# Attention items in ten steps, one step an iteration, with negated keys

## The chip, the cores and the metric

The kernel runs on one core of a Trainium2 chip. The metric is device time in microseconds (us) of one execution, the median of several; lower is better. In what follows PE is the matmul engine (TensorE), DVE is VectorE, ACT is ScalarE, POOL is GpSimd and SP issues the transfers (DMAs).

## What is computed

One block of an encoder over 1024 tokens of width 1024. Three branches mix the tokens, a merge and an output projection follow, and then sixteen experts. The change touches the two attention branches and what runs beside them:

```
# neighbourhood attention: 16 rows x 64 columns of tokens, 6 heads of 64
scores = einsum(q_r * dh**-0.5, k_win) + bias         # window 8 x 16 around each token
probs  = softmax(scores)
out    = einsum(probs, v_win)
# memory attention: 1024 tokens against 256 memory rows, 4 heads of 64
probs  = softmax(einsum(qh * dh**-0.5, kh));  out = einsum(probs, vh)
# the recurrent branch ends with a group norm over each head
y = ((y_sum - mean) * rsqrt(var + eps)) * ln_g + ln_b + bonus_sum;  y = y * g
merged = sum over the branches of sigmoid(gate) * (y_branch @ w_branch)
```

## The kernel before, in words

The program is a row of stages. A recurrent scan with projections beside it comes first; then the attention stage; then the merge of the three branches (helper `mm3`, L235 to L237), the output projection with the router, and the experts, whose weights take more than half of the time. Each stage uses its own buffers, partly at the addresses of the stage before, so the first loads of the merge (its weights, L1077, and its gates, L1110) wait until the buffers they land on are free.

The attention stage is written under a manual schedule: the order in which the Python loop calls the operations is the order on every engine. There are 40 items: 24 of neighbourhood attention (3 pairs of heads, 8 groups of 128 tokens) and then 16 of memory attention (2 pairs of heads, 8 groups). One item is two heads times 128 queries, and goes through these steps:

- score: six matmuls into `s` (PSUM, two banks an item, two buffers). For a neighbourhood item DVE then adds the bias and takes the row maximum in one custom instruction a head (L954, 288 or 384 keys), for a memory item it reduces 2x256 scores to two maxima (L1019). A small DVE instruction (L956, L1020) changes the maxima's sign.
- exp: ACT computes exp(score - maximum) with its row sum, one instruction a head (L908).
- recip: DVE inverts the two sums (L911).
- trans: PE transposes the probabilities into `tr` (L963, L1029), and ACT and DVE copy them out to `pt` (L967, L965, L1030).
- mix: PE multiplies by the values into `av` (L972, L1035; one PSUM bank, one buffer) and spreads the reciprocal sums over 64 rows by a small matmul (L920); ACT copies these to `rb` (L922).
- out: DVE forms y = av * rb (L926), ACT writes its rounded part `yh` (L928), POOL the remainder `yl` (L929).

The table `PIPE` says which step of which item an iteration calls, and in which order. Before, an iteration n does the out of item n-4, the exp of n-1, the recip and trans of n-2, the mix of n-3 and the score of n. So trans and mix of different items, and out and mix, meet in one iteration.

Two more things are threaded into the loop. Side generators prepare the next heads (`na_load`, `mem_load`: loads, a split of keys and queries into two parts on ACT and POOL, transposes of the values). The generator `group_norm` runs the recurrent branch's norm in six pieces, and is advanced twice an iteration from iteration 2 on. Its matmuls are the centring one (L816), the sums of squares (L822), the transposes of the inverse norm (L832) and the gate (L838); POOL adds the two directions (L808, L809), the bonus (L836), and writes the remainder of the result (L844).

Of the kernel before, what the change touches and what calls it, by code (L numbers as in the profile page):

```python
# [56 lines left out]
PIPE = (("out", 4), ("exp", 1), ("recip", 2), ("trans", 2), ("mix", 3), ("score", 0))  # L57
# [103 lines left out]
def block_kernel(ctx: ExitStack, tc: tile.TileContext, T, out, dbg=None, upto=99):  # L161
# [514 lines left out]
    def fill_gen():  # L676
        jobs = []
        for j0, j1, fn, sc_, dst in ((11, 14, AF.Copy, 0.125, pna[0:3]), (14, 17, AF.Copy, 1.0, pna[3:6]), (17, 20, AF.Copy, 1.0, pvc),
                                     (20, 22, AF.Copy, 0.125, pmq), (22, 46, AF.Tanh, 0.5, pgt)):
            jobs += [(j, fn, sc_, dst[j - j0]) for j in range(j0, j1)]  # L680
# [14 lines left out]
        def evac():  # L695
            while pend:
                p, n, s0 = pend.pop()
                _, fn, sc_, dst = jobs[n]
                if n == 3:
                    split_to(*(t[:, s0:s0 + 512] for t in kt0), p)  # L700
                    continue
# [84 lines left out]
    def group_norm():  # L786
# [17 lines left out]
        yield  # L804
        for n, (t0, j) in enumerate(its):
# [10 lines left out]
            PE.matmul(pcb, C("cent"), y0, start=True, stop=True)  # L816
            A.activation(y1, pcb, AF.Copy)
# [3 lines left out]
            for i in range(4):  # L821
                PE.matmul(pn[:, 2 * i:2 * i + 2], b1[:, i * 128:(i + 1) * 128], C("hsel"), start=True, stop=True)  # L822
            rn = gq.tile([128, 8], F32, name="grn", bufs=2)
# [7 lines left out]
            for i in range(4):  # L831
                PE.transpose(pb[:, i * 128:(i + 1) * 128], rb[:, 2 * i:2 * i + 2].rearrange("p h t -> p (h t)"), ident)  # L832
            V.tensor_mul(y1, y1, pb)
# [4 lines left out]
            PE.matmul(pg, g2[:, j * 128:(j + 1) * 128], lg[:, t0:t0 + 512], start=True, stop=True)  # L838
            yield
# [9 lines left out]
    def bias_load(m):  # L849
        if m < 6:  # L850
            bias[m] = ap.tile([128, 2, BOFF[3]], F32, name="bias", bufs=3)
            SP.dma_start(bias[m], T["rpb"][m // 2, m % 2])

    def na_load(j):
# [32 lines left out]
        for cg in range(4):  # L887
            p = abank("tr")
            w = NCOL[CTYPE[cg]]
            for i in range(4):  # L890
                PE.transpose(p[:4 * w, i * 128:(i + 1) * 128], VW[cg][:, 4 * i * w:4 * (i + 1) * w], ident)
            src, dst = p[:4 * w].rearrange("p (i c) -> p i c", i=4), VT[:4 * w, cg]
            if cg % 2:
                V.tensor_copy(dst, src)
                yield
            else:
                A.activation(dst, src, AF.Copy)

    def attention(score_of, trans_of, mix_of, tokens):
        o = {}  # L900

        def score():
            o["st"] = ap.tile([128, 8], F32, name="st", bufs=4)
            score_of(o)

        def exp():
            for h in range(2):
                A.activation(o["sb"][h], o["e"][h], AF.Exp, bias=o["st"][:, 2 + h:3 + h], scale=1.0, accum_out=o["st"][:, 4 + h:5 + h])  # L908

        def recip():  # L910
            V.reciprocal(o["st"][:, 6:8], o["st"][:, 4:6])  # L911

        def trans():
            trans_of(o)

        def mix():
            o["av"] = av = abank("av")
            mix_of(o, av)
            for h, q in enumerate((LO, UP)):
                PE.matmul(av[q, 128:256], o["st"][:, 6 + h:7 + h].to_broadcast([128, 64]), ident, start=True, stop=True)  # L920
            o["rb"] = rb = ap.tile([128, 128], F32, name="rb", bufs=2)
            A.activation(rb, av[:, 128:256], AF.Copy)  # L922

        def out():
            y = ap.tile([128, 128], F32, name="y", bufs=3)
            V.tensor_mul(y, o["av"][:, 0:128], o["rb"])  # L926
            y = tokens(y)
            A.activation(tokens(yh), y, AF.Copy)  # L928
            G.tensor_tensor(tokens(yl), y, tokens(yh).bitcast(F32), op=OP.subtract)  # L929
# [3 lines left out]
    def na_item(j, g):  # L933
# [11 lines left out]
        def score(o):  # L945
            KT, qb = na[j][:2]
            s, st = abank("s"), o["st"]
            for i, (a, b) in enumerate(((0, 0), (1, 0), (0, 1))):
                for h, q in enumerate((LO, UP)):
                    PE.matmul(s[:, h, :n], qb[a][q, rh, cg], grid(KT[b][q])[:, r0:r0 + NROW, c0:c0 + w], start=(i == 0), stop=(i == 2))  # L950
            sb = ap.tile([128, 2, 384], F32, name="sb", bufs=4)
            o["e"] = o["sb"] = [sb[:, h, :n] for h in range(2)]
            for h in range(2):
                V.tensor_tensor_reduce(out=sb[:, h, :n], in0=s[:, h, :n], in1=bias[2 * j + rh][:, h, b0:b0 + n],  # L954
                                       scale=1.0, scalar=-3.0e38, op0=OP.add, op1=OP.max, accum_out=st[:, h:h + 1])
            V.tensor_scalar(st[:, 2:4], st[:, 0:2], -1.0, None, op0=OP.mult)  # L956

        def trans(o):
            o["pt"] = pt = ap.tile([128, 2, 384], F32, name="pt", bufs=3)
            for h in range(2):  # L960
                p = abank("tr")
                for k in range(3):
                    PE.transpose(p[:m, k * 128:(k + 1) * 128], o["sb"][h][:, k * m:(k + 1) * m], ident)  # L963
                if h:
                    V.tensor_copy(pt[:m, h], p[:m, :384])  # L965
                else:
                    A.activation(pt[:m, h], p[:m, :384], AF.Copy)  # L967
# [7 lines left out]
        return attention(score, trans, mix, tokens)  # L975

    kb = [ap.tile([128, 2, NM], F32R, name=f"kb{v}") for v in "hl"]
    qm, vms = [], []

    def mem_load():  # L980
# [7 lines left out]
        A.activation(kb[0], kv[:, 0:2], AF.Copy)  # L988
        G.tensor_tensor(kb[1], kv[:, 0:2], kb[0].bitcast(F32), op=OP.subtract)
# [3 lines left out]
        for j in range(2):  # L993
# [5 lines left out]
            if j == 0:  # L999
                for m in range(2):  # L1000
                    p = abank("tr")
# [520 lines left out]
```

## Time and profile before

| | us |
|---|---|
| median of 3 runs | 2385.06 (2382.33 to 2385.69) |
| the profiled execution | 2382.75 |
| its span in the profile | 2380.9 |
| attention stage, first score to first matmul of the merge | 842.80 to 1018.60 |
| PE busy, share of the span | 94% |
| DVE, ACT, POOL busy | 70%, 55%, 26% |

The span runs from the first instruction to the last; 1.85 us of the execution lie outside it. A busy share is an average over stages, and the attention stage is where PE's share is lowest. In the rows below a bracket at the end of a line gives how long the engine sat idle before it, and what ended that.

### The profile page before, as it was taken

To read this page: it belongs to the slowest core of one execution; us is meant where nothing else is said; L and a number is where in the kernel's file an instruction comes from. 1 tells how busy PE (TensorE), PEld (TensorE's weight loads), DVE (VectorE), ACT (ScalarE), POOL (GpSimd) and SP (SyncE) were. 2 spreads that over 40 slices of the span, in tenths; PEclk is the share of its full clock that TensorE was granted. 3 is DMA by queue.
4 is the path that set the end of the run, shared out by engine and by line. 5 is a ranking of instruction groups with operands and counts; after the bars stand their busy time and mean duration, and the time that the engine had idled before them with its cause. 6 is when DMAs were issued, how large, how long until landed. Compare 5 with 4: busy or idle time off the path is not lost.

```text
span 2380.9 us, 33660 instructions
## 1 busy us (share of the span) xinstructions
PE 2235.4 (94%) x12614; PEld 1810.2 (76%) x12614; DVE 1666.4 (70%) x2012; ACT 1317.6 (55%) x1622; POOL 615.4 (26%) x1227
## 2 busy tenths in 40 slices
PE   7999999999999977799957999999999999999996
PEld 6677788877788855577846888888888888888885
DVE  6556556656656245664267888888888888888887
ACT  5554233433333355521235777777777777777775
POOL 1000566666666335343040000000000000000001
PEclk9999999999999988999978999999999999999998
DMA  6335444443442262165296999999999999999995
GB/s 236 151 142 208 114 117 130 126 122 95 133 128 77 90 220 97 36 193 188 90 348 237 376 380 388 387 391 385 390 380 381 379 392 387 389 387 389 379 350 195
DMA packets 196931, 594.20 MB, mean 250 GB/s; under 512 B 53408, under 2 KB 100768, under 8 KB 147616
## 3 DMA queue, kind: packets, MB, share of 16 engines
q1 hardware_dynamic: 190144, 568.62, 64.6%
q0 software_dynamic: 4752, 17.30, 2.7%
q10 hardware_dynamic: 1872, 6.13, 0.7%
q8 instruction: 99, 1.62, 0.3%
q14 instruction: 64, 0.52, 0.1%
HBM read 522.61 MB, written 69.39 MB: 249 GB/s over the span
## 4 chain that ended last, share of the span: by engine, by line
PE 72%; DVE 9%; POOL 8%; issue 3%; DMA 3%; ACT 2%; SPq 2%; POOLq 0%; DVEq 0%; ACTq 0%
PE y L1389 14%; PE acc L726 8%; PE g L1377 5%; PE g L1378 5%; PE g L1380 5%; PE u L1377 5%; PE u L1378 5%; PE u L1380 5%; PE acc L235 3%; POOL tmul L568 3%; PE acc L237 3%; PE acc L236 3%; POOL tinv L570 3%; PE tr L1437 1%; SPq L575 1%
## 5 line engine op out<-in xcount | busy, mean ns | idle before, releaser
L1354 DVE TENSOR_TENSOR ewl<-raw,ewh 128x2048 fp32r<-128x2048 f32 x380 | 849.7, 2284 | 6.5 <-ACT ewh L1349 6.5
L1349 ACT ACTIVATE ewh<-raw 128x2048 fp32r<-128x2048 f32 x380 | 720.7, 1914 | 113.8 <-PE u L1378 85.2
L1396 POOL DMA_INDIRECT acc<-ye,idx x15 | 43.4, 2894 | 950.1 <-DVE ye L1395 950.1
L726 PE MATMUL acc<-hlo,wh 128*128 128x512 f32 x560 | 224.8, 402 | 0.0
L726 PE MATMUL acc<-hhi,wh 128*128 128x512 f32 x560 | 224.6, 401 | 0.0
L726 PE MATMUL acc<-hhi,wl 128*128 128x512 f32 x560 | 224.5, 401 | 0.0
L568 POOL TENSOR_TENSOR tmul<-tinv,blk 96x60 f32<-96x60 f32 (+24 forms) x496 | 176.4, 356 | 147.8 <-DMA blk<-ldr 110.2
L1377 PE MATMUL g<-ewh,xh 128*128 128x512 f32 x512 | 206.6, 403 | 0.0
L1377 PE MATMUL u<-ewh,xh 128*128 128x512 f32 x512 | 202.2, 395 | 0.0
L1378 PE MATMUL g<-ewh,xl 128*128 128x512 f32 x512 | 201.0, 393 | 0.0
L1378 PE MATMUL u<-ewh,xl 128*128 128x512 f32 x512 | 199.5, 390 | 0.0
L570 POOL TENSOR_TENSOR tinv<-tinv,tmul 96x60 f32<-96x60 f32 (+24 forms) x496 | 174.6, 352 | 38.9
L1389 PE MATMUL y<-ewh,ah 128*128 128x512 f32 x512 | 137.8, 391 | 0.7 <-ACT ah L231 0.7
L1380 PE MATMUL g<-ewl,xh 128*128 128x512 f32 x512 | 137.4, 390 | 0.0
L1389 PE MATMUL y<-ewh,al 128*128 128x512 f32 x512 | 137.4, 390 | 0.0
L1380 PE MATMUL u<-ewl,xh 128*128 128x512 f32 x512 | 137.0, 389 | 0.0
L1389 PE MATMUL y<-ewl,ah 128*128 128x512 f32 x512 | 136.9, 389 | 0.0
L232 DVE TENSOR_TENSOR wl<-wraw,wh 128x1024 fp32r<-128x1024 f32 (+1 forms) x60 | 75.9, 1266 | 66.0 <-ACT wh L231 65.9
L726 PEld LDWEIGHTS acc<-hlo,wh 128*128 128x128 f32 x560 | 105.8, 189 | 20.5
L726 PEld LDWEIGHTS acc<-hhi,wl 128*128 128x128 f32 x560 | 105.7, 189 | 20.1
L726 PEld LDWEIGHTS acc<-hhi,wh 128*128 128x128 f32 x560 | 105.6, 189 | 20.1
L231 ACT ACTIVATE ah<-tr 128x512 fp32r<-128x512 f32 x64 | 38.4, 599 | 143.6 <-PE tr L1437 143.6
(315 smaller groups left out, 4359.7 us busy)
## 6 DMA issues: line engine op xcount, KB each, us to landing
raw<-in_wg_dram SPq DMA_DIRECT2D x128, 1024.0 KB
raw<-in_wu_dram SPq DMA_DIRECT2D x128, 1024.0 KB
raw<-in_wd_dram SPq DMA_DIRECT2D x128, 1024.0 KB
wraw<-in_wt_dram SPq DMA_DIRECT2D x46, 512.0 KB
pt<-pz SPq DMA_DIRECT2D x16, 768.0 KB
pgt<-po SPq DMA_DIRECT2D x48, 256.0 KB
gt<-pgt SPq DMA_DIRECT2D x16, 768.0 KB
blk<-ldr SPq DMA_DIRECT2D x64, 96.0 KB
```

What stands on the lines that cost most here:

```text
L232: V.tensor_sub(lo, src, hi.bitcast(F32))
L235: PE.matmul(out_, lh, rh, start=(k_ == 0), stop=False)
L236: PE.matmul(out_, ll, rh, start=False, stop=False)
L568: G.tensor_tensor(tm[:, 0:m, 0:n], tt[:, 0:m, j:j + 1].to_broadcast([4 * NB, m, n]), lt[:, j, None, j + 1:32].to_broadcast([4 * NB, m, n]) ...
L570: G.tensor_tensor(tt[:, 0:m, j + 1:32], tt[:, 0:m, j + 1:32], tm[:, 0:m, 0:n], op=OP.add)
L726: PE.matmul(p, l[:, k], r[:, k, s0:s0 + 512], start=(k == 0 and i == 0), stop=(k == KD - 1 and i == 2))
L1349: A.activation(hi, raws[seq[n]], AF.Copy)
L1354: V.tensor_sub(lo, raws.pop(seq[n]), his[seq[n]].bitcast(F32))
L1377: PE.matmul(p, xh[:, 4 * b + k], wh[:, k], start=(b == 0 and k == 0), stop=False)
L1378: PE.matmul(p, xl[:, 4 * b + k], wh[:, k], start=False, stop=False)
L1380: PE.matmul(p, xh[:, 4 * b + k], wl[:, k], start=False, stop=(b == 1 and k == 3))
L1389: PE.matmul(py[n], l[:, 2 * b + k], r[:, k, n * 512:(n + 1) * 512], start=(f == 0 and b == 0 and i == 0 and k == 0), stop=(f == 3 and b == ...
```

## The change

It changes four things.

1. An item's work is cut into ten steps (score, top, exp, trans, evac, mix, spread, mul, hi, lo), one an iteration, and an iteration calls the oldest item first: lo of n-9, hi of n-8, mul of n-7, spread of n-6, mix of n-5, evac of n-4, trans of n-3, exp of n-2, top of n-1, score of n. The loop has 50 iterations where it had 45. `spread` (the copy to `rb`) goes from ACT to DVE; a third of the memory items' copies out of `tr` goes from DVE to ACT.
2. The keys are stored negated (and the bias tables are negated once each, the first by DVE and the other five by POOL), so that the row statistic is the minimum of the negated scores. It enters exp as its bias directly, and the 40 instructions that changed the sign go.
3. PSUM is used otherwise: one `av` bank holds two items in two halves that take turns, two memory items share one `s` pair of banks, and the transposes of values go through `s` rather than `tr`. `st` has six buffers rather than four, `pt` two rather than three.
4. `group_norm` gets five more pauses a piece and one more at its start, so its six pieces have 86 pauses rather than 55. One of the two advances now comes ahead of the items' steps.

```diff
-PIPE = (("out", 4), ("exp", 1), ("recip", 2), ("trans", 2), ("mix", 3), ("score", 0))
+PIPE = (("lo", 9), ("hi", 8), ("mul", 7), ("spread", 6), ("mix", 5), ("evac", 4), ("trans", 3), ("exp", 2), ("top", 1), ("score", 0))
...
-        for j0, j1, fn, sc_, dst in ((11, 14, AF.Copy, 0.125, pna[0:3]), (14, 17, AF.Copy, 1.0, pna[3:6]), (17, 20, AF.Copy, 1.0, pvc),
+        for j0, j1, fn, sc_, dst in ((11, 14, AF.Copy, 0.125, pna[0:3]), (14, 17, AF.Copy, -1.0, pna[3:6]), (17, 20, AF.Copy, 1.0, pvc),
...
+    def negated(m):
+        if m in bias:
+            (G if m else V).tensor_scalar(bias[m], bias[m], -1.0, None, op0=OP.mult)
...
+    avs, turn = abank("av"), [0]
...
         def mix():
-            o["av"] = av = abank("av")
+            turn[0] ^= 256
+            o["av"] = av = avs[:, turn[0]:turn[0] + 256]
             mix_of(o, av)
...
+        def spread():
             o["rb"] = rb = ap.tile([128, 128], F32, name="rb", bufs=2)
-            A.activation(rb, av[:, 128:256], AF.Copy)
-
-        def out():
-            y = ap.tile([128, 128], F32, name="y", bufs=3)
-            V.tensor_mul(y, o["av"][:, 0:128], o["rb"])
-            y = tokens(y)
-            A.activation(tokens(yh), y, AF.Copy)
-            G.tensor_tensor(tokens(yl), y, tokens(yh).bitcast(F32), op=OP.subtract)
+            V.tensor_copy(rb, o["av"][:, 128:256])
+
+        def mul():
+            o["y"] = ap.tile([128, 128], F32, name="y", bufs=3)
+            V.tensor_mul(o["y"], o["av"][:, 0:128], o["rb"])
+
+        def hi():
+            A.activation(tokens(yh), tokens(o["y"]), AF.Copy)
+
+        def lo():
+            G.tensor_tensor(tokens(yl), tokens(o["y"]), tokens(yh).bitcast(F32), op=OP.subtract)
...
-                                       scale=1.0, scalar=-3.0e38, op0=OP.add, op1=OP.max, accum_out=st[:, h:h + 1])
-            V.tensor_scalar(st[:, 2:4], st[:, 0:2], -1.0, None, op0=OP.mult)
+                                       scale=1.0, scalar=3.0e38, op0=OP.add, op1=OP.min, accum_out=o["st"][:, h:h + 1])
...
+            if i % 2 == 0:
+                qs[0] = abank("s")
+            o["s"] = s = qs[0][:, :, i % 2 * NM:i % 2 * NM + NM]
...
-        for n in range(len(items) + 5):
+        live, extra, pend, negs = {}, [], [], (1, 3, 6, 10, 14)
+        for n in range(len(items) + 10):
...
+            if n >= GN0:
+                next(gn, 0)
             for part, lag in PIPE:
                 if n - lag in live:
                     live[n - lag][part]()
...
+            if n in negs:
+                negated(negs.index(n) + 1)
```

What this does to an iteration of neighbourhood attention on PE, before and after, in an iteration without a matmul of the group norm. In the kernel before (tr the transposes, av the mix and the spread reciprocals, s the scores; the numbers are those of the buffers):

```order
L963 MATMUL tr_9477<-cst_60,sb_9406 96x128 x3
L963 MATMUL tr_9482<-cst_60,sb_9406 96x128 x3
L972 MATMUL av_9487<-pt_9423,VT_9065 64x128 x6
L920 MATMUL av_9487<-cst_60,st_9340 64x128 x2
L950 MATMUL s_9499<-KTh_8803,qbh_8801 128x384 x2
L950 MATMUL s_9499<-KTh_8803,qbl_8802 128x384 x2
L950 MATMUL s_9499<-KTl_8804,qbh_8801 128x384 x2
```

In the changed kernel:

```order
L1001 MATMUL av_8741<-pt_9275,VT_8995 64x128 x6
L944 MATMUL av_8741<-cst_60,st_9145 64x128 x2
L992 MATMUL tr_9327<-cst_60,sb_9242 128x128 x3
L992 MATMUL tr_9328<-cst_60,sb_9242 128x128 x3
L979 MATMUL s_9341<-KTh_8798,qbh_8796 128x384 x2
L979 MATMUL s_9341<-KTh_8798,qbl_8797 128x384 x2
L979 MATMUL s_9341<-KTl_8799,qbh_8796 128x384 x2
```

The same matmuls stand there, but the mix has moved ahead of the transposes, and neighbouring groups belong to items one further apart: mix and transposes were one item apart and are two, transposes and scores were two apart and are three.

The same iteration on DVE. In the kernel before (y the output, st the statistics, pt the copy of the transposes, sb the biased scores):

```order
L926 TENSOR_TENSOR y_9024<-av_8992,rb_9001 128x128
L911 RECIPROCAL st_8950<-st_8950 128x2
L965 COPY pt_9031<-tr_9037 96x384
L954 ISA sb_9061,st_9053<-s_9054,bias_8783 128x384
L954 ISA st_9053 128x1
L954 ISA sb_9061,st_9053<-s_9054,bias_8783 128x384
L954 ISA st_9053 128x1
L956 TENSOR_SCALAR st_9053<-st_9053 128x2
```

In the changed kernel:

```order
L952 TENSOR_TENSOR y_9067<-av_8741,rb_9015 128x128
L948 COPY rb_9069<-av_8741 128x128
L996 COPY pt_9079<-tr_9030 96x384
L932 RECIPROCAL st_8983<-st_8983 128x2
L985 ISA sb_9094,st_9093<-s_9043,bias_8783 128x288
L985 ISA st_9093 128x1
L985 ISA sb_9094,st_9093<-s_9043,bias_8783 128x288
L985 ISA st_9093 128x1
```

The sign change at the end is gone, the copy to `rb` has come in behind the product, and the product now reads the `rb` of the iteration before.

The end of the stage on PE in the changed kernel (the gn matmul is the last gate matmul of the group norm, acc the first matmul of the merge):

```order
L837 MATMUL gn_10511<-cst_60,grb_10487 128x128 x4
L1070 MATMUL av_8741<-pt_10500,VT_9738 64x128 x4
L944 MATMUL av_8741<-cst_60,st_10408 64x128 x2
L1062 MATMUL tr_10531<-cst_60,sb_10482 128x128 x4
L844 MATMUL gn_10539<-lg_8819,g2_8817 128x512
L1070 MATMUL av_8741<-pt_10528,VT_9738 64x128 x4
L944 MATMUL av_8741<-cst_60,st_10442 64x128 x2
L1070 MATMUL av_8741<-pt_10553,VT_9738 64x128 x4
L944 MATMUL av_8741<-cst_60,st_10480 64x128 x2
L235 MATMUL acc_10622<-yh_8736,wh_10613 128x512
```

Before, the group norm's last matmul came in iteration 28 of 45; now it comes in iteration 43 of 50, and two mixes are all that stands between it and the merge.

## Rows read from the trace of the kernel before

**Rows 1.** The page's first part: busy time, share of the span, instructions.

```profile
PE 2235.4 (94%) x12614; PEld 1810.2 (76%) x12614; DVE 1666.4 (70%) x2012; ACT 1317.6 (55%) x1622; POOL 615.4 (26%) x1227
```

**Rows 2.** Stretches: PE, PEld, DVE, ACT, POOL busy (instructions), PEclk, DMA share, GB/s.

```profile
854.30:959.10 104.80, 83.11 (x698) 60.18 (x698) 53.99 (x183) 61.33 (x183) 52.85 (x56) 0.90 0.31 107
1000.00:1018.60 18.60, 14.00 (x154) 9.99 (x155) 11.57 (x34) 9.23 (x39) 3.65 (x8) 1.00 0.25 80
1018.60:1085.00 66.40, 64.53 (x281) 52.08 (x280) 42.51 (x53) 16.22 (x21) 30.53 (x23) 1.00 0.60 184
```

**Rows 3.** Waits from 842.8 to 1018.6: us in total, times, longest.

```profile
PE av L972 <- DVE y L926: 13.8, 12, 2.5
PE av L1035 <- DVE y L926: 6.9, 10, 1.2
```

**Rows 4.** Timeline, one memory item's iteration: start, us, engine, line, operation.

```profile
998.57 0.66 PE L1035 MATMUL av<-pt,VT 128*64 128x128 f32 x8 [0.60 <-DVE y L926]
...
999.37 0.38 PE L1018 MATMUL s<-kbh,qbh 64*128 64x256 f32 x2
...
999.92 0.66 PE L1029 MATMUL tr<-cst,sb 128*128 128x128 f32 x4
1000.03 0.69 DVE L1019 TENSOR_REDUCE st<-s 128x2 f32<-128x512 f32 x1 [0.86 <-PE s L1018]
...
1000.84 0.29 DVE L926 TENSOR_TENSOR y<-av,rb 128x128 f32<-128x128 f32 x1
...
1001.12 0.67 DVE L1030 COPY pt<-tr 128x512 f32<-128x512 f32 x1
...
1001.18 0.42 PEld L1035 LDWEIGHTS av<-pt,VT 128*64 128x64 f32 x8 [0.84 <-DVE y L926]
```

**Rows 5.** Timeline, neighbourhood items: what PE does from a mix on.

```profile
872.44 0.88 PE L972 MATMUL av<-pt,VT 96*64 96x128 f32 x12 [1.76 <-DVE y L926]
...
874.05 1.09 PE L891 MATMUL tr<-cst,VC 128*128 128x128 f32 x8
...
942.30 0.86 PE L963 MATMUL tr<-cst,sb 128*96 128x128 f32 x6
...
949.96 0.88 PE L972 MATMUL av<-pt,VT 96*64 96x128 f32 x12
...
951.72 0.44 PE L1003 MATMUL tr<-cst,kt 128*128 128x128 f32 x2
```

**Rows 6.** Timeline, PE at the four matmul groups of the group norm.

```profile
854.36 2.08 PE L816 MATMUL gn<-y,cst 128*128 128x512 f32 x2 [4.28 <-POOL y L808]
...
864.60 0.66 PE L832 MATMUL gn<-cst,grb 128*128 128x128 f32 x4 [1.13 <-ACT grb L828]
...
869.00 1.02 PE L838 MATMUL gn<-lg,g 128*128 128x512 f32 x2
...
947.92 1.13 PE L816 MATMUL gn<-y,cst 128*128 128x512 f32 x2 [0.84 <-POOL y L808]
...
951.99 0.95 PE L822 MATMUL gn<-cst,b 128*128 128x2 f32 x8
```

**Rows 7.** Groups by line and form, 842.8 to 1018.6: busy us, mean ns, idle before.

```profile
L929 POOL TENSOR_TENSOR yl<-y,yh 128x128 fp32r<-128x128 f32 x39 | 17.8, 457 | 43.1 <-ACT yh L928 43.1
...
L844 POOL TENSOR_TENSOR yl<-y,yh 128x512 fp32r<-128x512 f32 x6 | 7.6, 1270 | 9.6 <-ACT yh L843 9.6
L808 POOL TENSOR_TENSOR y<-y,y 128x512 f32<-128x512 f32 x6 | 7.6, 1270 | 3.3 <-DMA y<-yrw 3.3
...
L812 POOL TENSOR_SCALAR lg<-lg 128x1024 f32<-128x1024 f32 x1 | 1.0, 1046 | 0.0
```

**Rows 8.** Timeline, weight loads of 512 KB: a merge load's issue, and a later load.

```profile
983.11 12.78 SPq L1077 DMA_DIRECT2D wraw<-in_wbr_dram  x4
...
1043.27 0.34 SPq L1099 DMA_DIRECT2D wraw<-in_wout_dram  x1
...
1047.86 1.07 ACT L231 ACTIVATE raw<-wraw 128x1024 fp32r<-128x1024 f32 x1 [2.80 <-DMA wraw<-in_wout_dram]
```

More of the change, by code (lines that the diff above doesn't have):

```diff
@@ L699, in evac @@
                 if n == 3:
-                    split_to(*(t[:, s0:s0 + 512] for t in kt0), p)
+                    hi, lo = (t[:, s0:s0 + 512] for t in kt0)
+                    A.activation(hi, p, AF.Copy, scale=sc_)
+                    V.scalar_tensor_tensor(lo, p, sc_, hi.bitcast(F32), op0=OP.mult, op1=OP.subtract)
                     continue
@@ L886, in na_load, with v_out, attention, top @@
         na[j].append(VT)
-        for cg in range(4):
-            p = abank("tr")
-            w = NCOL[CTYPE[cg]]
[L890 to L899, printed above, removed]
+        for c2 in (0, 2):
+            p = abank("s")
+            for cg in (c2, c2 + 1):
+                w = NCOL[CTYPE[cg]]
+                for i in range(4):
+                    PE.transpose(p[:4 * w, cg - c2, i * 128:(i + 1) * 128], VW[cg][:, 4 * i * w:4 * (i + 1) * w], ident)
+            yield p, VT, c2
+    def v_out(p, VT, c2):
+        if c2 is None:
+            V.tensor_copy(VT, p[:, :, :NM])
+            return
+        for cg in (c2, c2 + 1):
+            w = NCOL[CTYPE[cg]]
+            (V.tensor_copy if cg % 2 else A.copy)(VT[:4 * w, cg], p[:4 * w, cg - c2].rearrange("p (i c) -> p i c", i=4))
+    avs, turn = abank("av"), [0]
+    def attention(score_of, top_of, trans_of, evac_of, mix_of, tokens):
         o = {}
         def score():
-            o["st"] = ap.tile([128, 8], F32, name="st", bufs=4)
             score_of(o)
+        def top():
+            o["st"] = ap.tile([128, 8], F32, name="st", bufs=6)
+            top_of(o)
         def exp():
             for h in range(2):
-                A.activation(o["sb"][h], o["e"][h], AF.Exp, bias=o["st"][:, 2 + h:3 + h], scale=1.0, accum_out=o["st"][:, 4 + h:5 + h])
-        def recip():
+                A.activation(o["sb"][h], o["e"][h], AF.Exp, bias=o["st"][:, h:h + 1], scale=-1.0, accum_out=o["st"][:, 4 + h:5 + h])
+        def trans():
             V.reciprocal(o["st"][:, 6:8], o["st"][:, 4:6])
-        def trans():
             trans_of(o)
+        def evac():
+            o["pt"] = ap.tile([128, 2, 384], F32, name="pt", bufs=2)
+            evac_of(o)
         def mix():
-            o["av"] = av = abank("av")
+            turn[0] ^= 256
+            o["av"] = av = avs[:, turn[0]:turn[0] + 256]
             mix_of(o, av)
@@ L973, in mix @@
                               start=(k == 0), stop=(k == 2))
-        return attention(score, trans, mix, tokens)
+        return attention(score, top, trans, evac, mix, tokens)
     kb = [ap.tile([128, 2, NM], F32R, name=f"kb{v}") for v in "hl"]
     qm, vms = [], []
+    qs = [None]
     def mem_load():
@@ L1036, in mix @@
                               o["pt"][:, h, m * 128:(m + 1) * 128], start=(m == 0), stop=(m == 1))
-        return attention(score, trans, mix, tokens)
+        return attention(score, top, trans, evac, mix, tokens)
     with tc.manual_schedule():
-        for _ in na_load(0):
-            pass
+        for v in na_load(0):
+            if v:
+                v_out(*v)
+        negated(0)
         for m in (1, 2):
```

75 lines of the change are left out of this document (42 added, 33 removed).

## The prediction, as written before the result

> **What bounds the kernel now.** I read the page first, then stretches, then waits, then the timeline. PE is busy 94% of the span [rows 1], so what matters is where it is not. The stretches show it: from 854.3 to 959.1, the neighbourhood items, PE works 83.1 of 104.8 us and its granted clock is 0.90; from 1000.0 to 1018.6, memory items alone, it works 14.0 of 18.6; in the merge behind, 64.5 of 66.4 [rows 2]. No other engine is near full in the attention stage: ACT has 61.3 and DVE 54.0 of the 104.8 us. So the stage is bound by a chain, not by an engine. The waits name it: the mix waits for DVE's product y, 12 and 10 times, up to 2.5 us [rows 3], beside waits of PE's weight loads for the same. The timeline shows why. A memory iteration takes 2.61 us, from 998.57 to 1001.18, in which PE works about 2.0. DVE reduces only when the scores end (0.86 us idle before it), and the product y of the item before, which frees the one `av` bank for the next mix, stands in DVE's queue behind that reduction. So scores, reduction, product and mix follow each other within one iteration [rows 4]. With a neighbourhood item the same wait was 1.76 us once [rows 5].
>
> **The change, part by part.** In the new order every step reads what earlier iterations made. I went through each engine's queue for what is left within one iteration. There are two such waits: mix(n-5) waits for DVE's spread(n-6), or at least mul(n-7), as the `av` bank is shared, and trans(n-3) waits for evac(n-4), as a neighbourhood item takes both `tr` banks. DVE reaches mul and spread right behind top(n-2) of the iteration before, which needs only scores that ended an iteration earlier; the mix itself gives the evac its time. So neither should stop PE, and PE's own work should set the pace. DVE's memory step is the nearest rival in length: 0.69, 0.67 and 0.29 [rows 4], 0.29 again for the copy that comes from ACT (estimated from the product of the same shape) and a small reciprocal, some 1.95 against PE's 2.01, and a third of the 0.67 copies go to ACT.
>
> PE's work, from rows without a wait inside:
>
> - A neighbourhood item: from a mix to what follows its scores 1.61 us (872.44 to 874.05, 288 keys) or 1.76 (949.96 to 951.72, 384 keys), half of the items each, and 0.86 for the transposes [rows 5]: 2.545 us, by 24 is 61.1.
> - A memory item: 1.35 (998.57 to 999.92) and 0.66 for the transposes [rows 4]: 2.01, by 16 is 32.2.
> - The group norm: 1.13 + 0.95 + 0.66 + 1.02 = 3.76 [rows 6], by 6 is 22.6.
> - The values' transposes for the later heads: four groups of 1.09 and two of 0.44 [rows 5], 5.2.
>
> That is 121.1 us. The start doesn't move: the first centring matmul waits at 854.36 for POOL's sum of data that lands late (4.28 us idle) [rows 6], and it stands there in the new order too. Ahead of it the new order has four scores and one item's transposes: with 0.55 for 256 keys (999.37 to 999.92) some 0.7 each, and 0.86, 3.7 us. The negation of the first bias table on DVE, at POOL's price below at most 2.0 us, lies before that wait and costs nothing; without it the first items would come that much later. So 117.4 us are left from 854.36, which ends PE's part at 971.8.
>
> Then the new waits:
>
> - POOL around iteration 10. In its queue stand the group norm's remainder and two sums (3 x 1.27), an item's lo (0.46), a bias table's negation (128x1920; from 1.05 for 128x1024 [rows 7] some 1.96), a key split of the 128x512 form (1.27) and the next lo (0.46): 7.96 us. The product two iterations later needs that lo, as `y` has three buffers. Behind it on DVE is the spread, and the mix waits for that: 8.5 us with 0.5 for these two. PE wants it after iterations 10 and 11, 2.55 and 2.55 + 1.13, at 6.2. I take the 2.3 us between.
> - Five more centring matmuls wait for POOL. Before, such a one waited 0.84 [rows 6]. Between 0 and 4.2 in all I take the middle, 2.
> - Side loads that land late, the slow clock after the wait at 854, the fill of the last steps: no row separates them. The bounds are 0 and 6; I take 2, as the durations above hold the matmuls' drain, which a stream hides.
>
> PE's last mix then ends at 978.1. **The hand-over** to the merge is dearer than before. Its first weights land on buffers of the group norm; the load was issued at 983.11, right behind the norm's last matmul [rows 8], and the merge began 35 us later without a wait. Now that matmul stands two mixes (0.80 each, 998.57 to 999.37 [rows 4]) ahead of the end. Of loads of that size one took 4.6 us from its issue to ACT's use (1043.27 to 1047.86), and the split of the first half is half of 1.07 [rows 8]: 4.6 + 0.5 - 1.6 = 3.5 us of idle PE. So the merge starts at 981.6 instead of 1018.6, 37 us earlier. The merge is PE's stream [rows 2] and what follows is issued relative to it, so the gain is kept. The key's scale of -1 and the split of the negated keys replace instructions of the same shape: nothing, and below nothing neither.
>
> The sum: the profiled execution took 2382.75, less 37.0 is 2345.75; I say 2346. The median of the three runs stands 2.3 us above that execution. About 4.8 us (0.2%) is what a measurement can tell from no change.
>
> **A rule that speaks against it.** The rows show each item with `av` and `s` banks to itself, so no run here shows two engines at one bank; the changed order lets PE score an odd memory item into banks in which DVE reduces the even one. The Trainium skill's "PSUM — Partial Sum Buffer" (section "Terms") says that no two of TensorE, ScalarE and VectorE may access one bank within one partition in the same cycle. By that rule, if such accesses take turns, the time is that of the first rival; by my reading of the order it is the sum.
>
> **The rivals.**
>
> - Banks take turns: the odd score waits out the even item's reduction, 8 times 0.69 [rows 4], 5.5 us, so 2351.5. For it: the two share banks. Against: in the new order no wait stands between them, and the reduction usually falls in the transposes ahead of the score. 0.08.
> - A wait is left in every iteration: as long as before in the memory items, 0.60 [rows 4], by 40 items 24 us, so 2370. For it: DVE's and PE's steps are near equal, and four queues in strict order pass on every delay. Against: every partner has most of an iteration's slack. 0.15, and a half of it is likelier than all.
> - PE's clock falls (slower). Place: the 117 us of small matmuls. The granted clock was 0.90 in the neighbourhood stretch and 1.00 among the memory items [rows 2], and PE stood idle in each iteration of both. If the new stream were granted a mean below 0.76, 117 x (1/0.76 - 1) = 37 us would be gone, and at the lower level (1.2 GHz, 0.5) the time would be 2346 + 117 = 2463. Against: the idle time shrinks, and the busiest stretch, the merge, has 1.00. 0.04.
> - It doesn't do what it says: a shared buffer ties the steps together again, and PE waits 1 us an iteration: no change, 2383. 0.03.
>
> **The numbers.** My forecast has 0.70; its own range is 2336 (no new wait, the weights hidden) to 2357. The range over the cases reaches from 2333, with drains hidden, to 2366, most of the second rival. Faster by over 0.2%: 0.70 + 0.08 + 0.15 = 0.93; within 0.2%: 0.03; slower: 0.04.
>
> **What would show it.** In the changed profile: the first centring matmul still near 854, the merge's first matmul at 978 to 990, PE busy over 90% of the stretch between; mixes no longer waiting for y, one wait of 2 to 3 us for POOL's lo around the tenth iteration, and 2 to 5 us of idle PE ahead of the merge, ended by the weights. I am wrong if PE is busy below 85% there, if DVE or ACT never rests, or if the granted clock is below 0.85.

## The result, and the profile after

The changed kernel takes 2367.52 us (median of 6 runs, 2362.52 to 2373.29) where the kernel before takes 2385.43: ratio 0.9925, interval 0.991 to 0.9941. It is faster, by 17.9 us, but the prediction was 2346 us with a range that ended at 2366. The profiled execution took 2365.71. PE's busy time over the whole execution is what it was in [rows 1]; the time saved is idle time. The page's first part:

```profile
PE 2235.4 (95%) x12614; PEld 1812.1 (77%) x12614; DVE 1659.5 (70%) x2007; ACT 1311.5 (55%) x1588; POOL 635.2 (27%) x1231
```

The first centring matmul starts at 855.08 (854.36 before, [rows 6]), the merge at 999.70 (1018.60 before). Stretches of the changed kernel, columns as in [rows 2]: first the stage from that matmul to the merge, then pieces of it, then the merge's first 7 us.

```profile
855.10:999.70 144.60, 123.44 (x1126) 89.67 (x1127) 79.14 (x274) 88.49 (x269) 90.42 (x86) 0.92 0.26 90
...
865.00:889.60 24.60, 19.95 (x196) 14.22 (x192) 13.24 (x50) 14.27 (x42) 18.18 (x10) 1.00 0.45 161
889.60:902.10 12.50, 10.96 (x68) 8.68 (x68) 5.68 (x24) 6.90 (x22) 11.22 (x11) 0.59 0.60 207
...
907.00:996.40 89.40, 78.09 (x778) 56.22 (x778) 55.35 (x184) 58.62 (x185) 45.76 (x56) 1.00 0.12 39
855.10:864.50 9.40, 9.40 (x44) 7.03 (x44) 2.25 (x10) 5.42 (x16) 9.40 (x5) 0.50 0.43 151
999.70:1007.00 7.30, 7.30 (x22) 5.54 (x23) 3.85 (x6) 1.51 (x3) 0.47 (x1) 0.68 0.76 261
```

PE is busy 123.4 of 144.6 us, 85%, where over 90% had been forecast. Two things stand out. PE is idle some 18 us before its last mix, and its granted clock is at the lower level (0.50, that is 1.2 GHz) from 855 to 864 and for most of 890 to 902, where every matmul takes nearly twice its time: both stretches lie behind idle time of PE, 1.24 us ahead of 855.08 behind 4.53 us ahead of 850.06, and 1.55 and 1.46 us at 889.68 and 892.20 (these two in a timeline further down). Not every wait has this behind it: PE waits 1.79 us at 912.86, and the granted clock from 907.00 to 996.40 is 1.00.

```profile
850.06 0.69 PE L979 MATMUL s<-KTh,qbh 64*128 64x384 f32 x2 [4.53 <-DVE st L985]
...
855.08 2.08 PE L819 MATMUL gn<-y,cst 128*128 128x512 f32 x2 [1.24 <-DVE st L985]
```

PE's largest waits from 855 to 1003 (us in total, times, longest), which answer to [rows 3]:

```profile
PE av L1001 <- DVE rb L948: 9.6, 8, 1.8
PE acc L235 <- ACT wh L231: 3.3, 1, 3.3
PE av L1070 <- DVE rb L948: 3.2, 4, 1.0
PE gn L819 <- POOL y L811: 1.7, 2, 0.8
PE gn L826 <- ACT b L822: 1.6, 1, 1.6
```

The mix's wait for the product y (20.7 us in 22 places before) is gone. A new one for the copy of the spread reciprocals, which stands behind the product on DVE, takes its place in 12. It has two main causes. The first, in a timeline of the changed kernel:

```profile
873.08 1.09 PE L904 MATMUL s<-cst,VC 128*128 128x128 f32 x8
...
874.21 0.58 ACT L913 COPY VT<-s 128x512 f32<-128x512 f32 x1 [3.13 <-PE s L904]
...
874.83 0.69 DVE L913 COPY VT<-s 96x512 f32<-96x512 f32 x1 [2.14 <-ACT VT L913]
...
875.44 0.28 DVE L952 TENSOR_TENSOR y<-av,rb 128x128 f32<-128x128 f32 x1
...
875.63 0.28 DVE L948 COPY rb<-av 128x128 f32<-128x128 f32 x1
...
875.97 0.88 PE L1001 MATMUL av<-pt,VT 96*64 96x128 f32 x12 [0.93 <-DVE rb L948]
```

The values' transposes are called at the end of an iteration, their copies at the head of the next, ahead of DVE's product and spread. So DVE, with 2.14 us of idle time, cannot begin its iteration until PE has ended the one before. The second cause, some 10 us on:

```profile
884.50 0.45 POOL L958 TENSOR_TENSOR yl<-y,yh 128x128 fp32r<-128x128 f32 x1
884.92 5.04 POOL L864 TENSOR_SCALAR bias<-bias 128x1920 f32<-128x1920 f32 x1
...
885.75 0.63 ACT L888 ACTIVATE KTh<-kt 128x512 fp32r<-128x512 f32 x1 [3.40 <-DMA kt<-pna]
...
889.68 1.05 PE L826 MATMUL gn<-cst,b 128*128 128x2 f32 x8 [1.55 <-ACT b L822]
...
889.95 1.26 POOL L889 TENSOR_TENSOR KTl<-kt,KTh 128x512 fp32r<-128x512 f32 x1
...
891.17 0.45 POOL L958 TENSOR_TENSOR yl<-y,yh 128x128 fp32r<-128x128 f32 x1
...
891.65 0.29 DVE L952 TENSOR_TENSOR y<-av,rb 128x128 f32<-128x128 f32 x1 [4.70 <-POOL yl L958]
891.86 0.28 DVE L948 COPY rb<-av 128x128 f32<-128x128 f32 x1
...
892.20 1.12 PE L1001 MATMUL av<-pt,VT 96*64 96x128 f32 x8 [1.46 <-DVE rb L948]
```

Between two remainders (884.50 and 891.17) POOL negates a bias table, for 5.04 us, and splits keys; the three y buffers are full, so DVE waits 4.70 us. In the same place ACT waits 3.40 us for a load of keys.

A smaller tie lies among the memory items. Two of them share a pair of `s` banks, and DVE's reduction of the odd one waits for ACT's exp of the even one, in seven of eight cases. The kernel before has no wait of this kind. The reduction stands ahead of DVE's product and spread, so one such case is part of a wait of the mix:

```profile
DVE st L1054 <- ACT sb L929: 8.4, 7, 2.0
...
957.80 0.69 DVE L1054 TENSOR_REDUCE st<-s 128x2 f32<-128x512 f32 x1 [0.64 <-ACT sb L929]
...
959.54 0.66 PE L1070 MATMUL av<-pt,VT 128*64 128x128 f32 x8 [0.94 <-DVE rb L948]
```

The hand-over came as forecast, 3.32 us of idle time ended by the weights, issued at 993.81 behind the group norm's last matmul (992.76):

```profile
993.81 0.81 SPq L1124 DMA_DIRECT2D wraw<-in_wbr_dram  x2
...
995.99 0.39 PE L944 MATMUL av<-cst,st 128*64 128x128 f32 x4
...
999.03 1.13 ACT L231 ACTIVATE wh<-wraw 128x512 fp32r<-128x512 f32 x2
...
999.70 0.79 PE L235 MATMUL acc<-yh,wh 128*128 128x512 f32 x1 [3.32 <-ACT wh L231]
```

### The profile page after: what moved, and what is told of

Its sections match the earlier page's. It is cut to its first block, busy times and chain, and to the rows that moved or that the text cites. A ratio compares the mean times of both kernels' runs of the same rounds, so it can differ in the third digit from the quotient of the medians.

```text
span 2363.9 us, 33649 instructions
## 1 busy us (share of the span) xinstructions
PE 2235.4 (95%) x12614; PEld 1812.1 (77%) x12614; DVE 1659.5 (70%) x2007; ACT 1311.5 (55%) x1588; POOL 635.2 (27%) x1231
## 4 chain that ended last, share of the span: by engine, by line
PE 51%; DVE 3%; DMA 1%; POOL 1%; ACT 1%; issue 1%; POOLq 0%; ACTq 0%; DVEq 0%
PE y L1436 14%; PE g L1424 5%; PE g L1425 5%; PE g L1427 5%; PE u L1424 5%; PE u L1425 5%; PE u L1427 5%; PE acc L235 2%; PE acc L237 1%; PE acc L236 1%; PE tr L1484 1%; PE tr L1414 1%; POOL m L1169 1%; PE pl L1256 1%; DVE ye L1342 0%
## 5 line engine op out<-in xcount | busy, mean ns | idle before, releaser
L568 POOL TENSOR_TENSOR tmul<-tinv,blk 96x60 f32<-96x60 f32 (+24 forms) x496 | 168.7, 340 | 150.8 <-DMA blk<-ldr 113.2
L570 POOL TENSOR_TENSOR tinv<-tinv,tmul 96x60 f32<-96x60 f32 (+24 forms) x496 | 179.7, 362 | 38.8
```

The costliest lines, as they stand in the source:

```text
L568: G.tensor_tensor(tm[:, 0:m, 0:n], tt[:, 0:m, j:j + 1].to_broadcast([4 * NB, m, n]), lt[:, j, None, j + 1:32].to_broadcast([4 * NB, m, n]) ...
L570: G.tensor_tensor(tt[:, 0:m, j + 1:32], tt[:, 0:m, j + 1:32], tm[:, 0:m, 0:n], op=OP.add)
```

## The experiments

All times are medians beside the kernel before on the same chip. Single executions of one kernel differ by up to 11 us, so a difference of some 3 us between two medians is not told apart; where intervals overlap the text says so. The runs were timed in groups, and the medians of the kernel before lie between 2383.8 and 2386.2 in them, so differences between groups are uncertain by some 2 us more. The edits are to the changed kernel unless the text names another; of long ones the main lines are shown. A profile is of one execution, and in these the first centring matmul starts anywhere from 853 to 859.

**Each suspected cost alone.** `e1_two_op` writes the negation in another form:

```diff
-            (G if m else V).tensor_scalar(bias[m], bias[m], -1.0, None, op0=OP.mult)
+            (G if m else V).tensor_scalar(bias[m], bias[m], -1.0, 0.0, op0=OP.mult, op1=OP.add)
```

> The bias negations on POOL are written with two operations (times -1, plus 0) where the change has one; nothing else differs. In the changed kernel one such negation takes 5.05 us (128x1920), the two-operation form of 128x1024 takes 1.04. Theory POOL (the negations hold up POOL's remainders lo, the three y buffers pass that on to DVE's product, and the mix waits): the negation takes about 1.96, the 1.5 us wait of the mix near 892 goes, and if the granted clock then stays up near 890 the 4 us lost there come back too: the merge starts 3 to 7 us before 999.7, time 2359 to 2363. Rival (the width sets the duration, not the form): 5.0 us again and 2366 to 2368. Rival (POOL is not what ends the waits): 1.96, but the merge starts within 1 us of 999.7.

Measured: 2365.68 us, 0.9912 (0.9897 to 0.9927), which overlaps that of the changed kernel. POOL's groups (busy us, mean ns), first of the changed kernel:

```profile
L864 POOL TENSOR_SCALAR bias<-bias 128x1920 f32<-128x1920 f32 x5 | 25.3, 5053 | 45.0 <-DMA bias<-in_rpb_dram 45.0
...
L815 POOL TENSOR_SCALAR lg<-lg 128x1024 f32<-128x1024 f32 x1 | 1.0, 1043 | 0.0
```

and of this run:

```profile
L864 POOL TENSOR_SCALAR bias<-bias 128x1920 f32<-128x1920 f32 x5 | 9.0, 1795 | 43.6 <-ACT VT L913 43.6
```

So the form sets the duration here, not the width alone: 1.80 us, near the 1.96 of the prediction. The wait near 892 is gone, yet the time hardly moves: ACT's wait for the keys stands at the same place (1.56 us at 890.25), and in the profiled execution the granted clock falls behind it all the same.

`e2_max` undoes the negation, of keys and bias tables, for both kinds of items:

```diff
-                (14, 17, AF.Copy, -1.0, pna[3:6])
+                (14, 17, AF.Copy, 1.0, pna[3:6])
...
-                                       scale=1.0, scalar=3.0e38, op0=OP.add, op1=OP.min, accum_out=o["st"][:, h:h + 1])
+                                       scale=1.0, scalar=-3.0e38, op0=OP.add, op1=OP.max, accum_out=o["st"][:, h:h + 1])
...
             top_of(o)
+            V.tensor_scalar(o["st"][:, 2:4], o["st"][:, 0:2], -1.0, None, op0=OP.mult)
```

> The negation alone is undone: keys and bias tables keep their sign, the statistic is the maximum again and DVE changes its sign by a small instruction behind each top (40 of them); the ten steps stay. Theory POOL: POOL loses 25 us of negations and DVE's first one, DVE gains 40 instructions of below 0.1 us with cover; the waits of the mix near 870 and 892 shrink or go, merge 4 to 8 us before 999.7, time 2357 to 2362. Rival (the sign changes stood on the path, and the negation is what the change gains from): slower than the changed kernel, 2369 to 2375. Rival (neither matters): 2366 to 2368.

Measured: 2362.74 us, 0.9896 (0.9882 to 0.991), 4.8 us below the changed kernel (the intervals touch), with the merge at 995.96. So the negation as it was written seems to cost some 5 us more than the 40 sign changes that it saves. The mixes' waits near 871 and 876 stay, as they are those behind the copies.

`e3_copies_late` moves the copies behind the steps:

```diff
-            for v in pend:
-                v_out(*v)
-            pend = []
             if n >= GN0:
...
             live.pop(n - 9, None)
+            for v in pend:
+                v_out(*v)
+            pend = []
```

> The copies of the values' transposes out of PSUM (ACT and DVE) are called behind the ten steps of an iteration rather than ahead of them. Theory copies (standing ahead of DVE's product and spread they wait for the last matmuls of PE's iteration before, so the next mix waits for the spread: 1.36, 0.93, 0.93, 1.79 and 1.18 us, the last for the memory rows' transposes): these five waits go, merge 5 to 6 us before 999.7, time 2360 to 2363. Rival (POOL would end those waits at nearly the same time): the waits change their releaser and 1 to 2 us are gained, 2364 to 2366.

Measured: 2358.88 us, 0.9887 (0.9873 to 0.9902). Four of the five waits are gone in its profile, the fifth is down to 0.74. That execution is at the upper end of its runs (2366.54): PE waits 1.92 us for the group norm's inverse norm, which POOL's negation had held up, and 3.21 us for the spread at 893.51. What PE gained it lost there to POOL.

`e4_y6` gives the product six buffers:

```diff
-            o["y"] = ap.tile([128, 128], F32, name="y", bufs=3)
+            o["y"] = ap.tile([128, 128], F32, name="y", bufs=6)
```

> The product y has six buffers rather than three. Theory POOL: DVE's product no longer waits for POOL's remainder lo (24.1 us in 12 waits, up to 4.7), so the mix's waits at 885.5, 892.2, 920.2, 959.5, 984.5 and 995.5 go, 6.3 us in all, and perhaps the 4 us of lower granted clock behind the one at 892: merge 6 to 10 us before 999.7, time 2356 to 2361. Rival (POOL or ACT itself is behind for good and more buffers only put the wait off): under 2 us, 2365 to 2367.

Measured: 2356.72 us, 0.9875 (0.986 to 0.9889), 10.8 us below the changed kernel: as expected of POOL, and the lowest of the single edits, though its interval overlaps that of `e3_copies_late`. The waits at 885.5, 892.2, 920.2, 964.6 and 984.5 (5.6 us) have no counterpart in its profile. Two more that the expectation names, at 959.5 and 995.5, stay (0.94 and 0.65), and those behind the copies are all there. The profiled execution is the slowest of its four (2363.07); PE waits 2.21 us in it for the inverse norm.

`e5_gn3` (hand-over) and `e6_load_order` (SP):

```diff
+            if n >= 20:
+                next(gn, 0)
             for g in list(extra):
```

> From iteration 20 on the group norm is advanced three times an iteration, so that its last matmul stands some six iterations earlier and the merge's first weights can be loaded while the memory items still run. Theory hand-over: the 3.3 us of idle PE ahead of the merge go, and the lower granted clock in the ten microseconds behind it (0.78 in the changed kernel, some 2 us) goes with them: 3 to 5 us, time 2362 to 2364. Rival (the group norm's denser steps cost the memory items as much in waits for POOL): within 1 us of the changed kernel.

```diff
-            if n in (4, 8, 12):
-                bias_load(n // 4 + 2)
...
                 elif v:
                     pend.append(v)
+            if n in (4, 8, 12):
+                bias_load(n // 4 + 2)
```

> The loads of the bias tables are issued behind the side generators' loads of the same iteration, not ahead of them. In the changed kernel SP stands from 855.5 to 877.6 in a bias load whose buffer is still read; the load of the next heads' keys behind it is issued at 879.7, ACT waits 3.4 us for it and PE 1.6 for ACT at 889.7. Theory SP: that wait goes, and the drop of the granted clock behind it more often than not: 1.6 to 6 us, time 2362 to 2366. Rival (the load is not late, ACT's wait had cover): 2367 to 2368.

Measured: 2370.13 us, 0.9929 (0.9916 to 0.9943), and 2365.54, 0.9916 (0.9901 to 0.9932). The first theory falls: the weights no longer stop the merge, but nine waits of the memory mixes for the spread, 6.7 us, have come in place of four (3.2 us). In the second run ACT no longer waits for the keys, and the mix at 893.97 waits 3.21 us behind POOL's negation instead: the two had covered each other.

**The steps themselves.** `e8_old_steps` undoes the ten lags on top of `e5_gn3`:

```diff
-PIPE = (("lo", 9), ("hi", 8), ("mul", 7), ("spread", 6), ("mix", 5), ("evac", 4), ("trans", 3), ("exp", 2), ("top", 1), ("score", 0))
+PIPE = (("mul", 4), ("hi", 4), ("lo", 4), ("exp", 1), ("trans", 2), ("evac", 2), ("mix", 3), ("spread", 3), ("score", 0), ("top", 0))
```

> The ten lags are undone and nothing else but the group norm's third advance (as in the run that has that alone): top in the score's iteration, exp 1, trans and evac 2, mix and spread 3, mul, hi and lo 4 behind; score and trans first called in the order of before. Theory steps: with evac and trans, top and score in one iteration again the mix waits again, 0.6 us and more an item, and the time is near that of before, 2378 to 2385. Rival (the two halves of the av bank, not the steps, took the wait away): within 4 us of the run with the third advance alone, 2362 to 2367.

Measured: 2382.95 us, 0.9991 (0.9982 to 1.0). The gain needs the steps; the two halves of `av` don't bring it alone: without the steps the mix waits for y again, scores for exp, and gate matmuls for DVE. The run does not price the steps by themselves, though: the scores' 5.4 us are all of odd memory items, behind the exp of the even one with which they now share a pair of banks, and the kernel before had no such wait. PE's largest waits in its profile, 855 to 1013:

```profile
PE gn L819 <- POOL y L811: 7.9, 5, 2.5
PE av L1001 <- DVE y L952: 7.0, 11, 1.2
PE s L1051 <- ACT sb L929: 5.4, 7, 2.2
PE gn L837 <- ACT grb L833: 4.0, 4, 2.2
PE gn L844 <- DVE y L839: 3.9, 4, 1.5
```

**Together.** `e7_all` is the sum of the edits of `e1`, `e3`, `e4`, `e5` and `e6`:

> All of these together: negations in two operations, copies behind the steps, six y buffers, three advances of the group norm from iteration 20 on, and bias loads behind the side loads. If the waits named so far are all there is, PE is busy over 95% from the first centring matmul to the merge, the granted clock falls no more between 870 and the merge, and the stage is 16 to 20 us shorter than in the changed kernel: time 2347 to 2352, where the prediction stood. If the clock falls without waits too, or if the waits only pass to another engine: 2354 to 2360.

Measured: 2353.07 us, 0.9859 (0.9841 to 0.9877), between the two cases of the expectation. `e9_four` leaves out the group norm's third advance:

> The run with all five edits without the group norm's third advance. Theory (the third advance puts two steps of one piece into one iteration, so that the memory items wait for its partners: in the run with all five, waits of 0.3 to 1.2 us in twelve places from 919 on, against 1.1 us of idle ahead of the merge that it saves): the waits from 940 on become those of the changed kernel or fewer, the idle of 3.3 us ahead of the merge comes back, and the time is within 2 us of the 2353.1 of that run, 2351 to 2355. Rival (the hand-over is worth more than those waits): 2355 to 2358.

Measured: **2347.11 us**, 0.9836 (0.9822 to 0.9849), better than either theory had it: the third advance seems to cost some 6 us (the intervals just overlap). With `e14_four_fill` below, from which it isn't told apart, this is the fastest version found, 38.5 us below the kernel before and 1 us from what was predicted for the change. Its stretches (the first from its first centring matmul to its merge):

```profile
858.70:982.10 123.40, 115.93 (x1126) 84.26 (x1126) 81.90 (x276) 88.32 (x269) 76.99 (x84) 0.98 0.30 101
858.70:864.00 5.30, 5.26 (x24) 3.56 (x24) 1.85 (x10) 5.10 (x14) 5.26 (x5) 0.61 0.87 306
866.00:980.00 114.00, 108.67 (x1082) 79.04 (x1080) 78.88 (x262) 81.41 (x251) 67.75 (x76) 1.00 0.25 84
```

and all of PE's waits from 858 to 983 that the view lists (the 4.1 us lie ahead of the first centring matmul):

```profile
PE gn L819 <- DVE st L985: 4.1, 1, 4.1
PE acc L235 <- ACT wh L231: 2.4, 1, 2.4
PE av L1070 <- DVE rb L948: 2.0, 4, 0.9
PE gn L819 <- POOL y L811: 1.9, 3, 0.8
PE gn L837 <- ACT grb L833: 1.0, 2, 0.6
```

The stage takes 123.4 us where the prediction had 127.2 (854.4 to 981.6) and the changed kernel 144.6. No neighbourhood mix waits any more, and the granted clock is 1.00 from 866 to 980.

`e10_tail` adds to `e9_four` the third advance, from iteration 34 on alone:

```diff
+            if n >= 34:
+                next(gn, 0)
             for g in list(extra):
```

> As the run with four edits, with the third advance of the group norm from iteration 34 on alone: its last matmul comes about three iterations earlier than in the changed kernel. Theory hand-over: the weights then land before the last mix, under 1 us of idle PE ahead of the merge, and fewer waits among the memory items than with the third advance from iteration 20: 2349 to 2352. Rival (the last piece's chain of ACT, DVE and POOL steps is as long as the three iterations): no better than the run with four edits.

Measured: 2353.53 us, 0.9864 (0.9849 to 0.988): the rival, and worse. Waits among the last memory items come back (1.18 for a mix, 1.18 and 0.78 for the norm's own steps), the merge's first matmul waits 1.80 us for DVE's product instead of 2.39 for the weights, and PE works 62.4 of the merge's first 65.7 us, where `e9_four` has 64.6 of 65.9. Why the merge itself is thinner was not tried.

`e13_two` has the edits of `e3` and `e4` alone, `e12_three_max` those of `e9_four` with the negation undone as in `e2_max` in place of its other form:

> Six y buffers and the later copies alone; negations of 5.05 us and the bias loads' place as in the changed kernel. Theory (these two take the waits of DVE's product, whatever holds POOL up; what is left is ACT's wait for the keys' load near 890 and POOL's late inverse norm near 870): 2350 to 2354. Rival (POOL's long negations still reach PE by another way, the group norm's inverse norm and the key split, with the granted clock falling behind it): 2355 to 2360.

> As the run with four edits, but with the negation undone (maximum and sign change) in place of the two-operation form. Theory (DVE has room: 82 of 123 us, and a sign change of below 0.1 us an item is hidden, as are POOL's 1.8 us negations): no difference beyond 2 us, 2345 to 2350. Rival (the sign change in DVE's queue comes ahead of the product and delays the mixes): 2351 to 2356. Rival (the negations still cost, at the start above all, where DVE's own holds up the first tops): 2341 to 2344.

Measured: 2352.76 us, 0.9872 (0.9857 to 0.9887), as the theory had it: six buffers and later copies carry 14.8 of the 20.4 us that `e9_four` gains on the changed kernel (by the ratios 12.6 of 21.2). Its profile has 5.6 us of waits for the inverse norm that POOL computes, where `e9_four` has 1.0. And 2350.25 us, 0.9853 (0.9838 to 0.9869), which overlaps `e9_four`: whether the negation gains anything once it is cheap is not settled; if so, it is some 3 us.

**The clock.** `e11_fill` puts unused matmuls into the changed kernel's first iterations, `e14_four_fill` into those of `e9_four`:

```diff
+            if n in (1, 3):
+                f = abank("gn")
+                for _ in range(8 if n == 1 else 3):
+                    PE.matmul(f, kt0[0][:, 0:128], kt0[0][:, 0:512], start=True, stop=True)
             for part, lag in PIPE:
```

> Into the changed kernel eleven matmuls (128x512, their result unused) are put in PE's first iterations, where PE stood idle 4.5 and 1.2 us before the first centring matmul; the output is the same. Theory clock (the granted clock falls to its lower level because PE idles there, and the 4 us that PE's work from 855 to 865 lost follow from it): the granted clock stays at 0.9 or more from 845 to 865, the part from the first centring matmul on is 3 to 5 us shorter, time 2363 to 2365. Rival (the clock is lower there for another reason, such as the transfers at that time, 400 GB/s): 0.5 again from 848 to 865, and the time is 0 to 3 us longer than that of the changed kernel.

> As the run with four edits, with the eleven unused matmuls in PE's first iterations. Theory clock: the granted clock is back at 1.0 by 860 and the stretch from the first centring matmul to the merge falls from 123.4 to 119 to 121 us; time 2343 to 2346. Rival (the work that PE does sooner there only waits for POOL's first inverse norm behind it): 2346 to 2348.

Measured: 2364.54 us, 0.9916 (0.9904 to 0.9929), and 2346.25, 0.9843 (0.9829 to 0.9856), neither told apart from the same kernel without them. The clock answers, though. In `e11_fill` PE works without a gap from 851.0 on, and its granted clock is:

```profile
851.00:857.40 6.40, 6.40 (x23) 4.23 (x24) 3.50 (x15) 5.43 (x17) 4.02 (x4) 0.54 0.94 348
857.40:868.00 10.60, 8.62 (x85) 6.72 (x83) 3.61 (x14) 4.99 (x15) 10.60 (x6) 1.00 0.29 97
```

1.00 from 857 where the changed kernel had 0.50 until 864. The time so won went into a wait: PE came 3.12 us too early for the group norm's inverse norm (869.28), which POOL computes behind a negation. In `e14_four_fill` the extra matmuls ran sooner, PE then idled 4.37 us ahead of the centring matmul, and the clock was 0.54 from 853 to 864 again; the stage took 126.0 us there (853.08 to 979.10) where 119 to 121 had been expected. Transfers at that time don't account for it: the clock was 0.89 in that run's 842 to 849, at 396 GB/s.

## Why the prediction was wrong

The direction and the mechanism held; the size did not, 17.9 us for 39. By its own steps, against the profiled execution:

- **Start and PE's work.** The first centring matmul stayed, 0.7 us later than before. PE's 117.4 us from there come out at 114.5: 141.3 us to the end of the last mix less 17.6 us of idle time and 9.2 us of lower clock (below). `e9_four` shows 115.9 busy directly, of which 2.05 are lower clock (0.61 in the first 5.26 busy us).
- **"There are two such waits"** was the step that failed first. There is a third: the copies of the transposed values, which the change moved to the head of an iteration, ahead of DVE's product, while their matmuls stand at the end of PE's iteration before. Five waits, 6.2 us. The prediction priced the transposes on PE (5.2) and not the queue in which their copies stand; `e3_copies_late` moves the copies, and four of the five waits go. Another wait within an iteration was missed too, that of an odd memory item's reduction for the even item's exp (8.4 us on DVE, 9.6 in `e9_four`); what it costs PE was not tried.
- **POOL around iteration 10, 2.3 us.** The waits at this place, 0.90 and 1.46, come to 2.4, but that is luck: the negation was priced at 1.96 from a row of another form (two operations) and took 5.05. What failed is that the delay was counted once: the three y buffers passed POOL's delays on in five places, 5.6 us, which six buffers took away. Four of the five lie behind the group norm's remainder and sums, which have nothing to do with the negation; the negation stands behind the one at 892.2.
- **Five centring matmuls, 2.0 us.** They waited 1.7.
- **Unplaced, 2.0 us** for late loads, the slow clock and the fill, bounded by 0 and 6. This was the largest miss. The keys' load, held up on SP behind a bias table's (issued at 879.71), cost 1.6 of PE's time; with the copies (6.2), the buffers (5.6) and the centring matmuls (1.7) that is 15 of the 17.6 us of idle time, and four waits of 0.3 to 0.9 are the rest. The lower clock is in 9.2 us more of PE's busy time: (1 - 0.50) of the 9.40 busy us from 855.1, and (1 - 0.59) of the 10.96 from 889.6. That is a term of the sum and not what a full clock would bring: in `e11_fill`, with 1.00 from 857 on, PE waited 3.12 us for POOL instead, and the time was not told apart. The prediction had a granted clock of 0.90 in [rows 2] and used it in a rival only; its durations were from full speed, so the clock belonged in the sum.
- **Hand-over, 3.5 us.** Measured 3.3. That the merge then begins at the lower clock (0.68 for 7 us) was not in it; from the merge to the end of the span the changed kernel takes 1364.2 us, 1.9 more than before.

With these terms the sum is 2345.75, plus 0.7 for the start, 11.3 for waits (17.6 less the 6.3 that were priced), 9.2 for the clock and 1.9 behind the merge's start, less 2.9 of PE's work and 0.2 at the hand-over: 2365.75. The profiled execution took 2365.71. It closes by construction, as PE's 114.5 us are what the other terms leave; the check on it is `e9_four`, with 113.88 (115.93 less 2.05).

Of the rivals, "a wait in every iteration" gave a time, 2370, near the measured one, with another mechanism: more than half of the iterations have none, and the others have causes of their own place. Banks taking turns, PE against DVE, had no occasion: no odd memory item's score ran beside the even item's reduction, and the eight odd ones took 0.39 and twice 0.27 to 0.29, like the even. The rule of the Trainium skill that was weighed there is thus neither borne out nor refuted. The clock rival was right that small matmuls behind a gap run slow, and wrong in size. Of the markers, first centring matmul, y, lo's wait (as 0.90 and 1.46 us) and hand-over came; the merge at 978 to 990 and PE at over 90% did not.

The total fits `e9_four`, whose four edits take away most of what the sum left out, but in part by luck: its stage is 3.8 us shorter than priced (123.4 for 127.2), it starts 4.3 later (858.7 for 854.4), and what follows the merge's start takes 1.2 more. So the size of PE's own work could be read from the trace of before; what the side effects of the change cost needed the position of every instruction that it moved, on each queue.

## What to carry to other kernels

When a pipeline is cut deeper, list for each engine which instruction of an iteration needs something made at the end of another engine's iteration before: one such instruction at the head of a queue (here the copies of the transposed values out of PSUM, in a few iterations) stops all the short steps behind it. Give the buffers between a steady engine and one with bursts of side work the depth of the burst, which here cost 1.5 KB a partition and brought some 11 us. And count a stretch's granted clock as a term of the sum, since idle time of PE can cost twice: once as waiting, and again in the matmuls behind it, as from 855 and from 890 here, though not behind the waits from 907 on.

## What the runs showed of the hardware

**POOL's one-operation form is slow.** A multiplication of 128x1920 f32 by one constant took 5.05 us on POOL, and the same with a second operation (plus 0) 1.80: 2.6 against 0.9 ns an element. The Trainium skill's "GPSIMD Engine Reference" (section "4.1 Engine selection") has operations with one input at roughly the line rate there. The nearest measure of that here is DVE's 1.15 us for the same width (`e1_two_op`, below): POOL's two-operation form took 1.6 times as long, its other form 4.4 times. The first comes nearer to that statement, the second does not agree with it, and the measurement decides.

**DVE waited for POOL inside an instruction.** DVE's own negation of the first bias table began while POOL's was running. In the changed kernel, timeline:

```profile
842.76 5.08 POOL L864 TENSOR_SCALAR bias<-bias 128x1920 f32<-128x1920 f32 x1 [44.35 <-DMA bias<-in_rpb_dram]
...
844.59 4.27 DVE L864 TENSOR_SCALAR bias<-bias 128x1920 f32<-128x1920 f32 x1
```

In `e1_two_op`, where POOL's had ended before:

```profile
841.57 1.79 POOL L864 TENSOR_SCALAR bias<-bias 128x1920 f32<-128x1920 f32 x1 [43.64 <-ACT VT L913]
...
843.79 1.15 DVE L864 TENSOR_SCALAR bias<-bias 128x1920 f32<-128x1920 f32 x1
```

4.27 us against 1.15, and it ended 1.02 us after POOL's (848.86 and 847.84), as it did in `e3_copies_late` and `e4_y6` too. No semaphore is shown between them. The Trainium skill's "SBUF — State Buffer" (section "Who interferes with whom") says that when DVE runs in a mode that uses two ports, which `tensor_scalar` can enter, it and POOL contend for a shared pair of ports: the instruction that is issued first holds them for its whole length, and the other is blocked. These rows agree: POOL's began first, and DVE's end follows POOL's by the same 1.02 us in all three kernels.
